# One hybrid decoder step on one core: fetch and split of the head outputs in two threads, whole value transposes, a new order of the column groups, and the inverse's small transfers on ScalarE's queue

## The chip, the core and the metric

The kernel runs on one core of a Trainium2 chip. Its engines work side by side, each through its own list of instructions in order: TensorE (PE, matmuls and transposes into PSUM), VectorE (DVE), ScalarE (ACT), GpSimd (POOL) and SyncE (SP, which here does nothing but issue DMA transfers). The metric is the time of one execution on the device in microseconds; lower is better. Before the change it is 1345.04 us, the median of three runs (1344.74 to 1347.03).

## The reference

One layer of a decoder that runs two mixers side by side on the same input of 2048 channels: RWKV-7 (16 heads of 64) and retention (8 heads of 128). There are 592 tokens: 16 meta tokens and 512 prompt tokens of one sequence, and 8 new tokens for each of 8 running sequences, which bring their own states.

```
z = einsum('btd,dn->btn', x, w_in)                 # 2048 -> 4224 (RWKV) + 4096 (retention) columns
o_a, s_a, shift = _rwkv7_mixer(z[..., :N_A_COLS], ...)   # per token: S <- S*w + (S·-kk) b^T + v k^T;  o = S·r
o_b, s_b = _retention_mixer(z[..., N_A_COLS:], ...)      # S <- g*S + k^T v, rotary q and k, group norm, gate
h = einsum('btc,cd->btd', concat([o_a, o_b]), w_out)     # 2048 -> 2048
y = layer_norm(ALPHA * x + h)
```

Everything is fp32. The new states of both mixers and the last projected row (`shift`) are outputs too.

## The kernel before

**Precision.** The two large products are done in three matmuls each, on a rounded high part and the remainder: `wh*XH`, `wh*XL` and `wl*XH`. ACT makes the high part (`wh<-raw`) and DVE the low part (`wl<-raw,wh`) of every weight chunk of 256 KB. Four such buffer pairs rotate; a chunk is loaded into one of three `raw` buffers by SP.

**Column groups.** The input projection runs over 65 column groups of 128 columns (`units`): one for the low-rank parts, then for each of eight pairs `p` (two RWKV heads, one retention head) the groups A k, r, v, g and B q, k, v, g. A group is four weight chunks, first over tokens 0 to 271 into `bank0`, then over the other 320 into `bank1`: 96 matmuls of 256 to 320 columns, then the next group. Evacuation of a bank (`gen_evac`) applies the token shift or the rotary factors. The rows `f32 ... 128x272` and `128x320` of the profile are these matmuls.

**Work of a pair beside it.** While TensorE goes through the groups, threads (Python generators) put their instructions between its matmuls:
- `gen_a(p)`: decays, keys, and the products of a chunk of 64 tokens; transposes of the values (`zsV`) into `Y` and `ZZ`; then a "bonus" product with `BD` that scales `zsV`.
- `gen_u(p)`: the inverse of a triangular 64 x 64 matrix for each chunk and head. The four 32 x 32 blocks go out to DRAM (`lt_d<-RW`, 4 transfers of 40 KB), come back spread over 120 partitions (`RW<-lt_d`, 3 of 160 KB), are inverted by 62 DVE instructions, and go back the same way (`tt_d<-RW`, 3 of 55 KB; `RW<-tt_d`, 4 of 40 KB).
- `gen_c(p)`: the chain over the nine chunks. Each link is matmul, ACT (`RHS`), matmul, DVE, matmul, DVE, and the next link needs the last result.
- `gen_s(p)`: the eight running sequences. `gen_f(p)`: group norm and gate of the RWKV output. `gen_b(h)`: retention head `h`, with `ron` as its output.

Outputs of pairs 0 to 6 are parked in DRAM (`o_d`). For the output projection `gen_o` fetches them again into five tiles, splits them into `xo` (in `XH`) and `xl`, and marks `o`. The last two, of pair 7, are taken from SBUF. The output projection has four column blocks `n` of 512, sixteen row blocks `k` and five token tiles `t`; for `n = 0` the first `EARLY = 14` row blocks are done for tiles 0 and 1 ahead of the rest (84 matmuls), and the rest of `n = 0` begins only when retention head 7 and the shift rows are done, since it needs their PSUM banks. The first 14 row blocks of `n = 0` take 196 matmuls in all, row block 14 another 14, and then row block 15 (pair 7's RWKV output) is needed.

**What sets the order.** Nothing is scheduled while the kernel runs. A planner (`Order`) keeps, as the program is built, an estimated clock for each engine, for PSUM and SBUF regions and for the DMA path, and places an instruction of a thread when its operands will be ready by the estimate and TensorE has come to that point. The estimates are in `Engine.cost`: before, a DVE instruction costs 68 ns + 1.04 ns a column whatever it is (but for `reciprocal`), an ACT instruction 93 (51 from PSUM) + 0.833. A transfer is taken to land 1300 ns + its bytes at 270 B/ns + 2400 ns (`LAND`) behind its issue. What is placed stays in that order on its engine, and an engine whose next instruction isn't ready waits. All transfers go through SP's list. `take` and `give` hand out three PSUM banks to the threads.

All ACT and DVE instructions of the threads carry line L380 in the profile, matmuls L403, transposes L409, DMA issues L420.

## Time and profile before

| | |
|---|---|
| median of three runs | 1345.04 us (1344.74 to 1347.03) |
| the profiled execution | 1345.04 us; 1343.3 us from its first to its last instruction |
| TensorE busy | 1309.4 us (97%) |
| VectorE busy | 879.8 us (65%) |
| ScalarE busy | 634.4 us (47%) |
| GpSimd busy | 55.3 us (4%) |
| mean DMA rate | 104 GB/s |
| granted TensorE clock | 0.997 |

The profiled execution's time is the median. The busy time of TensorE counts overlapping ends of pipelined matmuls, so how fast it is must be read from the distance between the starts of its instructions. An engine's idle time is listed by what ended it. DMA issues are seen on the queue of the engine that issues them (here SPq), with the time that the issue itself took; when the data landed is seen from who waited for it.

### The profile page before, as it was taken

Reading aid. Unit: us, or ns where it says so; the run is one execution under the profiler, and the core shown is the slowest. Engines: PE = TensorE matmul, PEld = TensorE weight load, DVE = VectorE, ACT = ScalarE, POOL = GpSimd, SP = SyncE. Lnnn points to the kernel's source line nnn. Section 1 sums busy time; section 2 is a strip of 40 time slices with the busy share of each in tenths; the row PEclk is TensorE's granted clock in tenths of the full one; section 3 lists DMA queues with packets and bytes.
Section 4 is the critical chain, followed back from the end, with each engine's and each line's share of the span. In section 5 each row is a group of like instructions: output and inputs, shape, how many; then the busy total and the mean of one; then the engine's idle time right before and its main releaser. Section 6 shows DMA issues by size and latency. Waiting matters only on the chain.

```text
span 1343.3 us, 27153 instructions
## 1 busy us (share of the span) xinstructions
PE 1309.4 (97%) x10488; PEld 1230.2 (92%) x10488; DVE 879.8 (65%) x2168; ACT 634.4 (47%) x1505; POOL 55.3 (4%) x117
## 2 busy tenths in 40 slices
PE   6999999999999999999999999999999998999995
PEld 6999999999999999999999999999999995777774
DVE  5765587658765876587658765876587658634258
ACT  4543654365536553655365536553655375512110
POOL 0000010000000010001000100010001000000002
PEclk9999999999999999999999999999999999999998
DMA  8343234322433243324332433243324356563224
GB/s 244 89 110 84 68 89 120 83 82 74 119 84 83 74 116 86 84 74 114 87 84 74 113 88 85 73 113 86 86 74 114 83 162 191 172 193 118 79 67 145
DMA packets 232344, 139.82 MB, mean 104 GB/s; under 512 B 58668, under 2 KB 212102, under 8 KB 231238
## 3 DMA queue, kind: packets, MB, share of 16 engines
q1 hardware_dynamic: 232214, 138.08, 36.2%
q8 instruction: 82, 1.34, 0.4%
q14 instruction: 48, 0.39, 0.1%
HBM read 119.30 MB, written 18.74 MB: 103 GB/s over the span
## 4 chain that ended last, share of the span: by engine, by line
PE 92%; DVE 5%; issue 1%; ACT 1%; DMA 0%; DVEq 0%; SPq 0%; ACTq 0%
PE bank L403 88%; PE bank L409 4%; DVE RW L380 3%; DVE wl L380 1%; DVE XL L380 1%; DMA RW<-in_x_prompt_dram 0%; DVE SHT L380 0%; ACT XH L380 0%; DVE XH L380 0%; ACT RT L380 0%; DVE RT L380 0%; ACT RSv L380 0%; ACT wh L380 0%; ACT SF L380 0%; ACT RHS L380 0%
## 5 line engine op out<-in xcount | busy, mean ns | idle before, releaser
L403 PE MATMUL bank<-XL,wh 128*128 128x320 f32 (+3 forms) x2080 | 631.3, 303 | 0.0
L403 PE MATMUL bank<-XH,wh 128*128 128x320 f32 (+3 forms) x2080 | 629.6, 303 | 1.2 <-ACT wh L380 1.2
L403 PE MATMUL bank<-XH,wl 128*128 128x320 f32 (+3 forms) x2080 | 626.1, 301 | 0.6 <-DVE wl L380 0.6
L403 PEld LDWEIGHTS bank<-XH,wh 128*128 128x128 f32 x2080 | 391.8, 188 | 3.6 <-ACT wh L380 1.4
L403 PEld LDWEIGHTS bank<-XH,wl 128*128 128x128 f32 x2080 | 392.0, 188 | 2.9 <-DVE wl L380 0.8
L403 PEld LDWEIGHTS bank<-XL,wh 128*128 128x128 f32 x2080 | 391.8, 188 | 2.9
L380 DVE TENSOR_TENSOR wl<-raw,wh 128x512 fp32r<-128x512 f32 x292 | 200.8, 689 | 156.2 <-ACT wh L380 151.8
L380 ACT ACTIVATE wh<-raw 128x512 fp32r<-128x512 f32 x292 | 183.8, 630 | 172.9 <-PE bank L403 145.6
L380 DVE TENSOR_TENSOR RW<-RW 120x84 f32<-120x84 f32 (+26 forms) x544 | 137.9, 256 | 18.5 <-DMA RW<-lt_d 4.1
L403 PE MATMUL bank<-RW 32*32 32x32 f32 (+6 forms) x2000 | 137.0, 239 | 4.8 <-DVE RW L380 4.7
L403 PEld LDWEIGHTS bank<-RW 32*32 32x32 f32 (+4 forms) x2000 | 109.8, 144 | 23.5 <-DVE RW L380 9.7
L380 ACT ACTIVATE RW<-bank 64x256 f32<-64x256 f32 (+8 forms) x218 | 93.2, 438 | 52.8 <-PE bank L403 29.1
L380 ACT ACTIVATE RT<-bank 64x320 f32<-64x320 f32 (+9 forms) x122 | 47.7, 397 | 114.0 <-DVE RT L380 72.6
L403 PE MATMUL bank<-more,XH 128*128 128x512 f32 (+1 forms) x250 | 75.9, 395 | 0.0
L380 ACT ACTIVATE SF<-RW,FT 64x64 f32<-64x64 f32 x144 | 49.4, 343 | 54.7 <-DVE RW L380 52.9
L403 PE MATMUL bank<-wh,XH 128*128 128x512 f32 x157 | 61.8, 396 | 0.0
L403 PE MATMUL bank<-wl,XH 128*128 128x512 f32 (+1 forms) x157 | 61.7, 395 | 0.0
L409 PE MATMUL bank<-CT,RW 128*128 128x128 f32 (+2 forms) x348 | 53.4, 283 | 8.3 <-DMA RW<-in_x_prompt_dram 7.6
L403 PEld LDWEIGHTS bank<-more,XH 128*128 128x128 f32 (+1 forms) x250 | 45.6, 183 | 12.6
L380 ACT ACTIVATE RW<-bank,OMM 128x272 f32<-128x272 f32 (+1 forms) x66 | 33.3, 504 | 45.6 <-PE bank L403 42.9
L403 PE MATMUL bank<-wh,XL 128*128 128x512 f32 x126 | 50.4, 400 | 1.4 <-DVE XL L380 1.4
L409 PEld LDWEIGHTS bank<-CT,RW 128*128 128x128 f32 (+2 forms) x348 | 42.0, 140 | 9.5 <-issue 7.6
(151 smaller groups left out, 1352.9 us busy)
## 6 DMA issues: line engine op xcount, KB each, us to landing
raw<-in_w_in_dram SPq DMA_DIRECT2D x259, 256.0 KB
raw<-in_w_out_dram SPq DMA_DIRECT2D x48, 256.0 KB
CT<-in_w_out_dram SPq DMA_DIRECT2D x30, 256.0 KB
RT<-in_state_ret_dram SPq DMA_DIRECT2D x8, 512.0 KB
out_dram<-RT SPq DMA_DIRECT2D x8, 512.0 KB
RW<-in_x_prompt_dram SPq DMA_DIRECT2D x16, 256.0 KB
out_dram<-RW SPq DMA_DIRECT2D x16, 256.0 KB
RW<-o_d SPq DMA_DIRECT2D x14, 288.0 KB
```

The source lines that it names most:

```text
L380: self.order.submit(Op(self.key, self.cost(name, n, kw, psum), reads, [out], lambda: f(*args, **kw)))
L403: lambda: self.eng.matmul(out, lhsT, rhs, start=start, stop=stop), (passes, move, load, shape, tiles)))
L409: lambda: self.eng.transpose(out, in_, ident), (1, move, _cols(in_) / 1.2, shape, tiles)))
```

## The change

- **Value transposes.** `zsV` was transposed in ten pieces of 64 tokens to 64 partitions of PSUM; now five pieces of 128 tokens go to all 128 partitions, and the even and odd chunks are copied from the two halves. ACT copies go from 9 to 12 a pair for the same elements.
- **Bonus product** as a thread of its own (`gen_bonus`, named X), started when the values are transposed. The next pair's r group and the gate of `gen_f` wait for it. The running sequences (`gen_s`) wait for `V` before they use `Y`.
- **Order of the column groups**: A k, r, then B q, k, v, g, then A v, g; in the last pair A k, r, B q, A v, B k, v, A g, B g.
- **The inverse's 14 small transfers a pair** are issued on ACT's queue. The constant `TI` stays on SP.
- **The planner's estimates**: DVE 82 ns instead of 68, a scan 2.08 ns a column instead of 1.04, ACT 107 and 68 instead of 93 and 51; a transfer on ACT's queue takes 480 ns of ACT and lands 900 ns (`LAND_OWN`) instead of 2400 ns after its bytes.
- **Fetch and split**: `gen_fetch` loads a parked output as soon as its own tile is free; `gen_o` splits.
- **The shift rows** wait for the last evacuation.

No computation is added or left out.

```diff
@@ -36,6 +36,7 @@
 LAND_BIG = 2400.0
+LAND_OWN = 900.0
 LD = 4
...
@@ -44,6 +45,8 @@
 EARLY = 14
+TURNS = "Ak Ar Bq Bk Bv Bg Av Ag"
+TURNS_LAST = "Ak Ar Bq Av Bk Bv Ag Bg"
 KEEP = ("A", 7, "g")
...
@@ -212,17 +215,19 @@
         self.clock[op.eng] = end
-        if op.eng in ("SP", "AQ"):
+        by = op.eng
+        if op.size and op.eng != "PE":
+            by = "SP"
             end = max(end + 1300.0, self.clock["DMA"]) + op.size / 270.0
             self.clock["DMA"] = end
-            end += LAND if op.size < 2e5 else LAND_BIG
+            end += LAND_OWN if op.eng == "ACT" else LAND if op.size < 2e5 else LAND_BIG
         for boxes, w in ((op.reads, False), (op.writes, True)):
...
                     l[:] = [x for x in l if x[6] > t]
-                l.append((p0, p1, c0, c1, w, op.eng, end))
+                l.append((p0, p1, c0, c1, w, by, end))
         op.emit()
...
@@ -356,10 +361,10 @@
         if self.key == "DVE":
-            return 68 + n * (6.3 if name == "reciprocal" else 1.04) + 57 * sum(
+            return 82 + n * {"reciprocal": 6.3, "tensor_tensor_scan": 2.08}.get(name, 1.04) + 57 * sum(
                 _is_ap(kw.get(k)) for k in ("scalar", "scalar1", "scalar2"))
         if self.key == "ACT":
-            return (51 if psum else 93) + n * 0.833 + 93 * sum(_is_ap(kw.get(k)) for k in ("scale", "bias"))
+            return (68 if psum else 107) + n * 0.833 + 93 * sum(_is_ap(kw.get(k)) for k in ("scale", "bias"))
         if kw.get("op") == ALU.pow:
...
@@ -430,7 +435,7 @@
     S = Dma(nc.sync, "SP", od)
-    S2 = Dma(nc.scalar, "AQ", od)
+    S2 = Dma(nc.scalar, "ACT", od)
     until, mark, stage = od.until, od.mark, od.stage
...
@@ -752,16 +757,27 @@
         G.memset(Y[64:128, 1, 9, :], 0.0)
-        for c0, c1 in ((0, 4), (4, 8), (8, 10)):
+        for g0, g1 in ((0, 4), (4, 5)):
             bb, = yield from take()
-            b = bb.rearrange("p (c n) -> p c n", c=4)
-            n = c1 - c0
-            for c in range(c0, c1):
-                T.transpose(b[0:64, c - c0, :], zsV[:, 64 * c:64 * c + 64], ident)
-            act(ZZ[64:128, c0:c1], b[0:64, 0:n].rearrange("p c (h v) -> p c h v", h=2))
-            act(Y[64:128, 0, c0:c1, :], b[0:64, 0:n, 0:64])
-            act(Y[0:64, 1, c0:c1, :], b[0:64, 0:n, 64:128])
+            b = bb.rearrange("p (g n) -> p g n", g=4)
+            for g in range(g0, g1):
+                T.transpose(b[:, g - g0, :], zsV[:, 128 * g:128 * g + 128], ident)
+            for e in range(2):
+                own, cs = b[64 * e:64 * e + 64, 0:g1 - g0], slice(2 * g0 + e, 2 * g1, 2)
+                act(ZZ[64:128, cs], own.rearrange("p g (h v) -> p g h v", h=2))
+                act(Y[64:128, 0, cs, :], own[:, :, 0:64])
+                act(Y[0:64, 1, cs, :], own[:, :, 64:128])
             give(bb)
+        mark(f"V{p}", 1)
+        od.call(lambda: od.start(f"X{p}", gen_bonus(p), 2))
+        yield from until((f"U{p}", 99))
+        b, = yield from take()
+        yield from gen_c(p, b)
+        give(b)
+        od.call(lambda: od.start(f"F{p}", gen_f(p), 2))
+        yield
+
+    def gen_bonus(p):
         yield from hold()
...
@@ -773,13 +789,6 @@
         give(b0, b1)
-        mark(name, 3)
-        yield
-        yield from until((f"U{p}", 99))
-        b, = yield from take()
-        yield from gen_c(p, b)
-        give(b)
-        od.call(lambda: od.start(f"F{p}", gen_f(p), 2))
         yield
...
@@ -812,22 +821,22 @@
             h, q = k // 2, k % 2
-            S.dma_start(out=lt_d[p % 2][k].rearrange("c s t -> s c t"),
+            S2.dma_start(out=lt_d[p % 2][k].rearrange("c s t -> s c t"),
                         in_=LT[64 * h + 32 * q:64 * h + 32 * q + 32, :, 32 * q:32 * q + 32])
...
         for g in range(3):
-            S.dma_start(out=SUB3[40 * g:40 * g + 40], in_=lt_d[p % 2].rearrange("k c s t -> (k c) s t"))
+            S2.dma_start(out=SUB3[40 * g:40 * g + 40], in_=lt_d[p % 2].rearrange("k c s t -> (k c) s t"))
         for j in range(31):
...
         for g in range(3):
-            S.dma_start(out=tt_d[p % 2].rearrange("k (m g) i -> k m g i", g=3)[:, :, g, :], in_=TI[40 * g:40 * g + 40])
+            S2.dma_start(out=tt_d[p % 2].rearrange("k (m g) i -> k m g i", g=3)[:, :, g, :], in_=TI[40 * g:40 * g + 40])
         mark(f"U{p}", 2)
...
             h, q = k // 2, k % 2
-            S.dma_start(out=TT[64 * h + 32 * q:64 * h + 32 * q + 32, :, 32 * q:32 * q + 32],
+            S2.dma_start(out=TT[64 * h + 32 * q:64 * h + 32 * q + 32, :, 32 * q:32 * q + 32],
                         in_=tt_d[p % 2][10 * k:10 * k + 10, 0:32].rearrange("c j i -> j c i"))
...
@@ -879,6 +888,7 @@
         give(tr)
+        yield from until((f"X{p}", 99))
         tt(on, on, zsV[:, 64:640], ALU.add)
...
@@ -908,6 +918,7 @@
         act(RSs, n0[:, 256:384])
+        yield from until((f"V{p}", 1))
         mm(n0[:, 384:512], AR_[:, 1728:1856], Y[:, :, 9, :])
...
@@ -1060,7 +1071,7 @@
                     if half == 0 and p:
-                        yield from until((f"A{p-1}", 1 if s == "k" else 3) if s in "kr" else (f"F{p-1}", 99))
+                        yield from until({"k": (f"A{p-1}", 1), "r": (f"X{p-1}", 99)}.get(s, (f"F{p-1}", 99)))
                     zs, i = {"r": (zsR, 0), "k": (zsK, 1), "v": (zsV, 2), "g": (zsG, 3)}[s]
...
@@ -1094,7 +1105,7 @@
     for p in range(NPAIR):
-        units += [("A", p, s) for s in "krvg"] + [("B", p, s) for s in "qkvg"]
+        units += [(x[0], p, x[1]) for x in (TURNS if p < NPAIR - 1 else TURNS_LAST).split()]
...
@@ -1263,26 +1274,37 @@
+        def gen_fetch():
+
+            for i in range(KO - 2):
+                t, kt = otk[i % 5], korder[i]
+                if t is TA:
+                    yield from until((f"S{NPAIR-1}", 1))
+                elif t is Z0:
+                    yield from until(("evac", 2 * len(units)))
+                else:
+                    yield from until((f"U{NPAIR-1}", 2))
+                if i >= 5:
+                    yield from until(("o", i - 4))
+                yield from until((f"{'F' if kt < 8 else 'B'}{kt % 8}", 99))
+                S.dma_start(out=t[:, 0:576], in_=o_d[kt])
+                mark("fetch", i + 1)
+                yield
+
         def gen_o():
...
-            yield from until((f"U{NPAIR-1}", 2), (f"S{NPAIR-1}", 1), (f"A{NPAIR-1}", 3), ("evac", 2 * len(units) - 8))
-
-            for ki in range(KO + 5):
-                if ki >= 5:
-                    k = ki - 5
+            for k in range(KO):
+                if k < KO - 2:
+                    yield from until(("fetch", k + 1))
                     t = otk[k % 5][:, 0:576]
-                    if k >= KO - 2:
-                        yield from until((f"B{NPAIR-1}", 99), (f"{'F' if k == KO - 1 else 'B'}{NPAIR-1}", 99))
-                        t = Y_[:, 64:640] if k == KO - 1 else ron
-                    yield from until(("event", n_in - 4 + min(3, (640 * k + 639) // TOK // 4) + 1))
-                    act(xo[:, k, 0:576], t)
-                    tt(xl[:, k, 0:512], t[:, 0:512], xo[:, k, 0:512].bitcast(F32), ALU.subtract)
-                    tt(xo[:, k, 576:640], t[:, 512:576], xo[:, k, 512:576].bitcast(F32), ALU.subtract)
-                    mark("o", k + 1)
-                if ki < KO - 2:
-                    kt = korder[ki]
-                    yield from until((f"{'F' if kt < 8 else 'B'}{kt % 8}", 99))
-                    S.dma_start(out=otk[ki % 5][:, 0:576], in_=o_d[kt])
+                else:
+                    yield from until((f"X{NPAIR-1}", 99), (f"B{NPAIR-1}", 99), (f"{'F' if k == KO - 1 else 'B'}{NPAIR-1}", 99))
+                    t = Y_[:, 64:640] if k == KO - 1 else ron
+                yield from until(("event", n_in - 4 + min(3, (640 * k + 639) // TOK // 4) + 1))
+                act(xo[:, k, 0:576], t)
+                tt(xl[:, k, 0:512], t[:, 0:512], xo[:, k, 0:512].bitcast(F32), ALU.subtract)
+                tt(xo[:, k, 576:640], t[:, 512:576], xo[:, k, 512:576].bitcast(F32), ALU.subtract)
+                mark("o", k + 1)
...
@@ -1337,7 +1359,7 @@
         def gen_shift():
-            yield from until((f"B{NPAIR-1}", 99))
+            yield from until((f"B{NPAIR-1}", 99), ("evac", 2 * len(units)))
             rows = SHO.rearrange("p s i -> p (s i)")
...
@@ -1353,6 +1375,7 @@
+        od.start("fetch", gen_fetch(), OPRIO)
         od.start("o", gen_o(), OPRIO)
```

What moves on the engines, at two places. The first is a round of the inverse in an odd pair. Before, SP issues its last transfers among the loads of the weight chunks (`raw`):

```order
L420 DMA raw_100<-in_w_in_dram 128x4x128
L420 DMA tt_d_127<-RW 440x1x32 x2
L420 DMA raw_101<-in_w_in_dram 128x4x128
L420 DMA raw_99<-in_w_in_dram 128x4x128
L420 DMA raw_100<-in_w_in_dram 128x4x128
L420 DMA tt_d_127<-RW 440x1x32
L420 DMA RW<-tt_d_127 32x10x32 x4
```

Now they stand in ACT's list, among the splits (`wh`) and the copies of retention:

```order
L425 DMA tt_d_127<-RW 440x1x32
L385 ACTIVATE RT<-RT 32x128 x2
L385 ACTIVATE wh_104<-raw_101 128x512
L385 ACTIVATE XH<-RT 32x128 x2
L385 ACTIVATE RT<-RT 32x128 x2
L385 ACTIVATE RT<-bank_116 128x320
L425 DMA tt_d_127<-RW 440x1x32
L385 ACTIVATE wh_105<-raw_99 128x512
L425 DMA RW<-tt_d_127 32x10x32 x4
L385 ACTIVATE RW<-bank_115,OMM 128x272
L385 ACTIVATE RW<-bank_115 128x272
```

Between the last store of the round and the loads that need it stands one split in the pairs 1, 3 and 5, six instructions with two splits in the pairs 2, 4 and 6, and two copies of a bank in pair 7. Behind the loads stand the copies of the next bank and the next split.

The second place is TensorE's list where the output projection has begun and the chain of pair 7 isn't finished. Before, these are the rows around the 84th matmul of the output projection (`bank0` and `bank1` with 512 columns; `RW` and `RHS,RW` are the chain, `CT,RT` the transposes of retention head 7, `CT,SHO` the shift rows, `64x64` the end of the chain):

```order
L403 MATMUL bank_115<-wh_105,XL 128x512
L409 MATMUL bank_121<-CT,RT 128x128 x4
L409 MATMUL bank_122<-CT,RT 128x80
L403 MATMUL bank_115<-wl_109,XH 128x512
L403 MATMUL bank_117<-RW 128x128
L403 MATMUL bank_117<-RHS,RW 66x128
L409 MATMUL bank_121<-CT,SHO 33x128
L409 MATMUL bank_121<-CT,SHO 88x128
L403 MATMUL bank_117<-RW 128x128
L409 MATMUL bank_121<-CT,SHO 88x128 x2
L403 MATMUL bank_120<-RW 64x64 x26
```

Now the transposes of head 7 stand behind 5 matmuls of the output projection instead of 83, and the shift rows behind 13 instead of 84:

```order
L408 MATMUL bank_115<-wh_102,XL 128x512
L414 MATMUL bank_121<-CT,RT 128x128 x4
L414 MATMUL bank_122<-CT,RT 128x80
L408 MATMUL bank_115<-wl_106,XH 128x512
L408 MATMUL bank_117<-RW 128x128
L408 MATMUL bank_119<-wh_103,XH 128x512
L408 MATMUL bank_119<-wh_103,XL 128x512
L408 MATMUL bank_119<-wl_107,XH 128x512
L408 MATMUL bank_115<-wh_103,XH 128x512
L408 MATMUL bank_115<-wh_103,XL 128x512
L408 MATMUL bank_115<-wl_107,XH 128x512
L408 MATMUL bank_118<-RW 128x128
```

The end of the chain (`64x64`) stands behind 84 of these matmuls before and behind 140 now; the transposes after the group norm of pair 7 behind 118 and behind 174.

## The prediction

> **What bounds the kernel now.** I read the page first, then the stages, then TensorE's waits. The page has TensorE busy all the time, and it owns the chain that ended last:
>
> ```profile
> span 1343.3 us, 27153 instructions
> PE 1309.4 (97%) x10488; PEld 1230.2 (92%) x10488; DVE 879.8 (65%) x2168; ACT 634.4 (47%) x1505; POOL 55.3 (4%) x117
> PE 92%; DVE 5%; issue 1%; ACT 1%; DMA 0%; DVEq 0%; SPq 0%; ACTq 0%
> ```
>
> So a gain must come from TensorE's own work or from places where TensorE waits; ACT, with 47%, has room, but only on average. By stages (span, then busy time of PE, PEld, DVE, ACT, POOL):
>
> ```profile
> 550.00:600.00 50.00, 49.55 (x463) 47.17 (x462) 37.72 (x94) 33.03 (x90) 1.57 (x3) 1.00 0.24 68
> 1100.00:1150.00 50.00, 43.32 (x271) 32.65 (x270) 42.41 (x93) 32.65 (x71) 4.13 (x4) 1.00 0.62 183
> 1150.00:1200.00 50.00, 50.00 (x218) 39.54 (x217) 25.35 (x40) 17.90 (x30) 0.00 (x0) 1.00 0.67 213
> ```
>
> A pair in the middle loses 0.45 us, the stretch where the last pair's chain meets the output projection 6.68 us, the output projection nothing. The waits of TensorE over the whole span, and then those between 1100 and 1150 us:
>
> ```profile
> PE bank L403 <- DVE RW L380: 4.7, 8, 1.1
> PE bank L403 <- ACT RHS L380: 2.8, 3, 1.3
> PE bank L403 <- DVE XL L380: 1.4, 3, 0.9
> PE bank L409 <- ACT RT L380: 0.4, 1, 0.4
> ...
> PE bank L403 <- DVE RW L380: 2.1, 2, 1.1
> ```
>
> The second set has the other three rows unchanged. So 2.1 + 2.8 + 1.4 + 0.4 = 6.7 us are lost in that stretch, and 4.7 - 2.1 = 2.6 us in 8 - 2 = 6 waits before it, one a pair, 0.44 us each. What the start and the end cost (loading x, the last norm and store) the change leaves as it is. The profiled execution's own time is 1345.04 us, 1.7 us more than its span, and is the median; sums below start from it.
>
> **The change, part by part.**
>
> *Value transposes.* What five transposes fewer a pair save is read from distances between starts, in pair 5's beginning:
>
> ```profile
> 619.38 0.60 PE L409 MATMUL bank<-CT,RW 128*128 128x128 f32 x4
> 619.73 0.36 PE L403 MATMUL bank<-XH,wl 128*128 128x258 f32 x1
> 619.93 0.28 PE L403 MATMUL bank<-XH,wh 128*128 128x258 f32 x1
> ...
> 622.38 0.60 PE L409 MATMUL bank<-CT,RW 128*64 128x128 f32 x4
> 622.74 0.36 PE L403 MATMUL bank<-XH,wh 128*128 128x258 f32 x1
> 622.94 0.28 PE L403 MATMUL bank<-XL,wh 128*128 128x258 f32 x1
> 623.06 0.28 PE L403 MATMUL bank<-XH,wl 128*128 128x258 f32 x1
> ```
>
> Four transposes of 64 columns and the matmul behind them take 622.94 - 622.38 = 0.56 us; a 258-column matmul alone takes 623.06 - 622.94 = 0.12; so the four cost 0.44, or 0.11 each. Four with 128 columns cost 619.93 - 619.38 - 0.12 = 0.43: the same. Ten become five: 5 x 0.11 = 0.55 us a pair, 8 x 0.55 = 4.4 us. All of it is TensorE's time in stages where it is 99 to 100% busy, so it counts in full, as long as nothing else comes to bound the pair. The three copies more on ACT (12 for 9) lie under TensorE's work (ACT's share is 47%).
>
> *The planner's price of a scan.* The wait in each middle pair has this in front of it:
>
> ```profile
> 577.82 1.52 DVE L380 TENSOR_TENSOR_SCAN RW<-CT,RW 128x657 f32<-128x657 f32 x1
> ...
> 712.43 1.52 DVE L380 TENSOR_TENSOR_SCAN RW<-CT,RW 128x657 f32<-128x657 f32 x1
> ...
> 580.98 0.28 DVE L380 TENSOR_TENSOR RW<-bank,N 64x128 f32<-64x128 f32 x1
> ...
> 581.32 0.49 PE L403 MATMUL bank<-RW 128*128 128x128 f32 x2 [0.45 <-DVE RW L380]
> ```
>
> The second scan row, from the next pair, gives the period: 712.43 - 577.82 = 134.6 us. The scan took 1.52 us; the old price is 68 + 657 x 1.04 = 751 ns, so the planner put the chain's matmul some 0.77 us too early behind it. The new price is 82 + 657 x 2.08 = 1449 ns. TensorE has matmuls of the column groups to do meanwhile, so the 2.6 us go; bounds 0 (another instruction is as badly priced) and 2.6. I take 2.6.
>
> *Last pair and output projection.* Before, 83 of the 84 early matmuls stand ahead of head 7's transposes, and the chain's last links wait one after another with nothing to put between. DVE is full there:
>
> ```profile
> 1120.00:1130.00 10.00, 7.48 (x45) 5.12 (x43) 9.79 (x22) 6.47 (x14) 1.75 (x2) 1.00 0.52 155
> ```
>
> Now head 7 is done earlier (its q group is third in the pair, and its transposes stand behind 5 output matmuls), the banks of tiles 2 to 4 come free, and the chain's links have 140 matmuls around them instead of 84. One takes 0.23 us:
>
> ```profile
> 1321.01 0.40 PE L403 MATMUL bank<-wh,XL 128*128 128x512 f32 x1
> 1321.24 0.40 PE L403 MATMUL bank<-wl,XH 128*128 128x512 f32 x1
> ```
>
> 56 x 0.23 = 12.9 us of fill for 2.1 + 2.8 + 0.4 = 5.3 us of waits for the chain and the shift rows. I take those as gone. The 1.4 us for XL I keep: the split can only begin when the last column group has read XH, which no earlier fetch alters. Bounds 0 and 6.7, taken 5.3.
>
> What is late next? Row block 15 needs pair 7's output. From the copy of the chain's result to the end of its split:
>
> ```profile
> 1140.43 0.60 ACT L380 ACTIVATE RW<-bank 128x512 f32<-128x512 f32 x1 [1.51 <-PE bank L403]
> ...
> 1155.19 0.69 DVE L380 TENSOR_TENSOR XL<-RW,XH 128x512 fp32r<-128x512 f32 x1
> ```
>
> that is 1155.88 - 1140.43 = 15.5 us. Before, 210 - 84 = 126 output matmuls (29 us) covered it. Now 70 are left, 70 x 0.23 = 16.1 us, and 0.55 for five transposes among them: 16.7. The margin is 1.2 us. Without it TensorE stands for what the norm is late; I take 0, at worst 2 us.
>
> *The inverse's transfers on ACT.* What SP paid:
>
> ```profile
> L420 SPq DMA_DIRECT2D lt_d<-RW x32: 331/452/1143, 77.6 to 1023.4; - x32
> L420 SPq DMA_DIRECT2D RW<-lt_d x24: 307/326/328, 81.2 to 1026.3; - x24
> L420 SPq DMA_DIRECT2D RW<-tt_d x32: 332/450/464, 122.9 to 1068.1; - x32
> L420 SPq DMA_DIRECT2D tt_d<-RW x24: 788/814/1352, 113.4 to 1063.5; - x24
> SPq L420 <- DMA tt_d<-RW: 15.6, 8, 2.2
> SPq L420 <- DMA lt_d<-RW: 0.8, 3, 0.3
> ```
>
> A pair's 14 issues come to 4 x 0.452 + 3 x 0.326 + 4 x 0.450 + 3 x 0.814 = 7.0 us of ACT, which makes its 634 us 690. The waits, 2.0 us a pair for `tt_d` (at most 2.2) and at most 0.3 for `lt_d`, now hold ACT. Queued behind them are splits, copies of the two projection banks and the chain's `RHS` and `SF`. How long may a split be late?
>
> ```profile
> 534.93 0.63 ACT L380 ACTIVATE wh<-raw 128x512 fp32r<-128x512 f32 x1 [1.12 <-PE bank L403]
> 536.69 0.63 ACT L380 ACTIVATE wh<-raw 128x512 fp32r<-128x512 f32 x1 [1.12 <-PE bank L403]
> 537.35 0.69 DVE L380 TENSOR_TENSOR wl<-raw,wh 128x512 fp32r<-128x512 f32 x1 [0.64 <-ACT wh L380]
> ```
>
> TensorE frees a buffer every 1.76 us and comes back to it three chunks later, after 5.3 us; the split takes 0.63 + 0.69 = 1.3 us and 0.1 between. So 3.9 us are to spare. The worst hop is `tt_d`, 2.2 of wait and 4 x 0.45 = 1.8 of issue, 4.0 us, less what a split between them uses up. That is 0.1 us over for each of 8 pairs, 0.8 us; the other hop (0.3 + 3 x 0.326 = 1.3 us) is covered. Bounds 0 and 0.8 by these rows; I take 0.8. SP loses waits among the weight loads, but no wait of TensorE names a weight load, so I credit nothing.
>
> *Bonus thread, order of the groups, separate fetch.* The bonus product has the group A k of the next pair (some 17 us) before A r needs its tile; no instruction is added. The values now come as the seventh group, right before the chain, where before they lay ready early; TensorE has groups to do until then. I take 0, between -1 and +2 us (one wait of 0.25 us a pair).
>
> *Sum.* 1345.0 - 4.4 - 2.6 - 5.3 + 0.8 = 1333.5 us.
>
> **The rivals.**
>
> A: *The stretch at the end keeps its waits.* For it: DVE's 9.79 of 10 us there: a full engine isn't helped by more fill. Against: the same DVE work is now spread over 12.9 us more of matmuls, and head 7 lies earlier. Price: the 5.3 us stay, and of the rest nothing changes: 1338.8 us.
>
> B: *ACT's wait eats the gain.* The point is 3.9 us from the last split on time. For it: in the first pair DVE stood 4.1 us for such a transfer:
>
> ```profile
> 88.29 0.87 DVE L380 TENSOR_TENSOR RW<-RW 120x31 f32<-120x31 f32 x4 [4.11 <-DMA RW<-lt_d]
> ```
>
> A wait as long on ACT, with 1.8 us of issue, is 5.9 us, 2.0 us over. In one hop a pair: 8 x 2.0 = 16 us in place of the 0.8, so 1345.0 - 12.3 + 16 = 1348.7 us. In both hops it would be 1365. It decides from 12.3 / 8 = 1.5 us over the margin a pair. Against: that wait had two weight loads of 256 KB queued ahead, and at the ACT hops SP never waited over 2.2 us.
>
> C: *Two queues hold each other up at the issue.* So far SP alone issues. If each of the four `RW<-tt_d` issues on ACT lasted one SP issue longer, that is 4 x 0.45 = 1.8 us a pair beyond the 0.1, and 1345.0 - 12.3 + 8 x 1.9 = 1347.9 us. For it: no row excludes it. Against: SP is left with a weight load of 0.4 us or so every 134.6 / 32 = 4.2 us, so most ACT issues meet none. The Trainium skill (Perfetto Trace Analysis, "DMA Instruction — HWDGE (DVE, Sync)") states the rule behind this: an issuing sequencer waits for its semaphores first and then locks the descriptor generator for its exclusive use. With one issuer before, no run here shows it yet.
>
> D: *Nothing to be seen.* The new prices are only other errors: each middle pair gets one wait of 0.5 to 1 us elsewhere (8 x 0.75 = 6 us), and the end keeps its waits: 1338.8 + 6 = 1344.8 us. For it: 14 ns more on each DVE instruction is far from exact. Against: with prices half as good there was one wait a pair.
>
> **How the numbers follow.** Forecast 50%, A 25%, D 13%, B 7%, C 5%. The forecast's own range is 1331 (XL's 1.4 us and ACT's 0.8 go too) to 1337.5 (2 us for row block 15 and 2 for the new order come). For 8 in 10 the range goes down to 1330, since transfers freed of SP's list may gain a little, and up past A to 1345. A measurement here tells about 0.2%, 2.7 us, from no change. Faster by more than that (below 1342.3): forecast, A and a third of D, 0.79. Within it: the rest of D and a third of C, 0.11. Slower: B and the rest of C, 0.10.
>
> **What would show it.** In the profile after: TensorE's waits for DVE RW near zero in the middle pairs, and a stretch of 10 us without `[... <-DVE RW]` behind the scan; 40 transposes fewer, all of 128 columns; a pair's period shorter by about 1 us; PE's idle time of 6.7 us around the last chain down to 1 to 2 us; ACT's waits for `tt_d` near 2 us a pair, with no wait of PE for `wh` or `wl`. Wrong it is if PE waits for `wh` or `wl` in each pair (B or C), if PE still waits for RHS at the end (A), or if row block 15 makes a new gap before the second column block.

## The result, and the profile after

The changed kernel took 1323.24 us (median of four runs, 1322.62 to 1324.24), the kernel before beside it 1345.15 us (1344.74 to 1347.03): ratio 0.9835, 95% interval 0.9818 to 0.9852. That is 21.9 us less, where 11.5 were forecast. The direction was right, the size was not; the time lies below the range of 1330 to 1345.

The page of the changed kernel (span; busy time and share of each engine; the chain that ended last by engine):

```profile
span 1322.0 us, 27007 instructions
PE 1297.2 (98%) x10448; PEld 1225.3 (93%) x10448; DVE 881.1 (67%) x2168; ACT 634.6 (48%) x1529; POOL 56.8 (4%) x117
PE 92%; DVE 4%; DMA 1%; ACT 1%; issue 1%; POOL 1%; ACTq 0%; SPq 0%; DVEq 0%; POOLq 0%
```

Its stages, the same three stretches as before (span, then busy time of PE, PEld, DVE, ACT, POOL):

```profile
550.00:600.00 50.00, 50.00 (x463) 48.84 (x463) 33.76 (x89) 31.09 (x89) 0.20 (x1) 1.00 0.30 82
1100.00:1150.00 50.00, 49.73 (x288) 39.14 (x287) 36.19 (x73) 31.49 (x66) 2.00 (x2) 1.00 0.62 195
1150.00:1200.00 50.00, 50.00 (x217) 39.61 (x216) 18.21 (x28) 10.35 (x17) 0.00 (x0) 1.00 0.51 161
```

And all waits of its TensorE that the view lists:

```profile
PE bank L414 <- DMA RW<-in_x_prompt_dram: 7.9, 2, 7.6
PE bank L408 <- ACT wh L385: 1.2, 1, 1.2
PE bank L408 <- DVE wl L385: 0.9, 2, 0.6
PE bank L414 <- DVE XL L385: 0.6, 1, 0.6
```

What is left is the program's start and one wait of 0.26 us for `wl` at 1111.5 us. The rows for `DVE RW` (4.7 us), `ACT RHS` (2.8), `ACT RT` and the projection's `XL` are gone; the stretch around the last chain, which lost 6.68 us, loses 0.27.

The length of a pair is read from TensorE itself: every kernel has the same 6240 products of the input projection, 96 for each column group, so the first product of a pair is found by counting. The first and the last of the eight pairs begin, before (with one product more, to show the distance of two starts), at

```profile
35.81 0.28 PE L403 MATMUL bank<-XH,wh 128*128 128x272 f32 x1
966.63 0.29 PE L403 MATMUL bank<-XH,wh 128*128 128x272 f32 x1
966.75 0.29 PE L403 MATMUL bank<-XL,wh 128*128 128x272 f32 x1
```

and after, at

```profile
36.91 0.28 PE L408 MATMUL bank<-XH,wh 128*128 128x272 f32 x1
955.65 0.38 PE L408 MATMUL bank<-XH,wh 128*128 128x272 f32 x1
```

So the span's 21.3 us divide as follows.

| stretch | before | after | measured | forecast |
|---|---|---|---|---|
| start to the first pair | 35.8 | 36.9 | +1.1 | 0 |
| seven pairs | 930.8 | 918.7 | -12.1 | -(7 x 0.55 + 5 x 0.44) = -6.1 |
| last pair's start to the end | 376.6 | 366.3 | -10.3 | -(0.55 + 0.44 + 5.3) = -6.3 |

(The forecast's +0.8 for ACT's queue was spread over the pairs; of the six waits behind a scan, five lie in the seven pairs and one in the last.) From the third to the seventh, the pairs took 134.6 us each; now they take 132.6 to 132.9. VectorE's scan, from which the prediction took the period, is no good ruler after the change: it stands 131.9 and 133.6 us apart in turn, since its place within the pair changes.

### The profile page after: what moved, and what is told of

It is laid out like the page before. It is cut to its first block, busy times and chain, and to the rows that moved or that the text cites. A ratio compares the mean times of both kernels' runs of the same rounds, so it can differ in the third digit from the quotient of the medians.

```text
span 1322.0 us, 27007 instructions
## 1 busy us (share of the span) xinstructions
PE 1297.2 (98%) x10448; PEld 1225.3 (93%) x10448; DVE 881.1 (67%) x2168; ACT 634.6 (48%) x1529; POOL 56.8 (4%) x117
## 4 chain that ended last, share of the span: by engine, by line
PE 92%; DVE 4%; DMA 1%; ACT 1%; issue 1%; POOL 1%; ACTq 0%; SPq 0%; DVEq 0%; POOLq 0%
PE bank L408 89%; PE bank L414 4%; DVE RW L385 2%; DVE XL L385 1%; POOL MOM L385 1%; DMA RW<-in_x_prompt_dram 0%; DVE SHT L385 0%; DVE wl L385 0%; DMA tt_d<-RW 0%; DVE RT L385 0%; DVE MOM L385 0%; ACT RT L385 0%; ACT XH L385 0%; ACT RW L385 0%; ACT wh L385 0%
## 5 line engine op out<-in xcount | busy, mean ns | idle before, releaser
L408 PE MATMUL bank<-RW 32*32 32x32 f32 (+6 forms) x2000 | 133.8, 237 | 0.0
L385 ACT ACTIVATE RW<-bank 64x64 f32<-64x64 f32 (+8 forms) x242 | 96.2, 411 | 52.2 <-PE bank L408 25.3
L414 PE MATMUL bank<-CT,RW 128*128 128x128 f32 (+3 forms) x308 | 47.4, 281 | 8.5 <-DMA RW<-in_x_prompt_dram 7.9
L414 PEld LDWEIGHTS bank<-CT,RW 128*128 128x128 f32 (+3 forms) x308 | 38.1, 146 | 9.9 <-issue 7.6
```

Source lines behind the costliest of these rows:

```text
L385: self.order.submit(Op(self.key, self.cost(name, n, kw, psum), reads, [out], lambda: f(*args, **kw)))
L408: lambda: self.eng.matmul(out, lhsT, rhs, start=start, stop=stop), (passes, move, load, shape, tiles)))
L414: lambda: self.eng.transpose(out, in_, ident), (1, move, _cols(in_) / 1.2, shape, tiles)))
```

## What the middle of the program gained, row by row

The third to the seventh pair fell from 134.62 us to 132.78 on average, 1.84 us each. Two parts were foreseen. The transposes take 0.55 us less. The wait behind the scan is gone; it cost more than its listed 0.44. From the start of the wide product ahead of it (580.57) to the waiting one (581.32, shown above) 0.75 us passed, where two such starts stand 0.15 apart, so 0.60. The listed wait only begins where the product ahead ends, 0.30 after its start, though in a full stream the next one starts before that end. The two products ahead:

```profile
580.42 0.31 PE L403 MATMUL bank<-XH,wl 128*128 128x320 f32 x1
580.57 0.30 PE L403 MATMUL bank<-XH,wh 128*128 128x320 f32 x1
```

A third part was not foreseen. Before, a group of eight products of 64 rows (16 passes) was cut by one wide product in the third and each later pair, six times:

```profile
605.02 0.93 PE L403 MATMUL bank<-RW 64*128 64x128 f32 x10
605.88 0.39 PE L403 MATMUL bank<-XH,wh 128*128 128x272 f32 x1
606.20 0.71 PE L403 MATMUL bank<-RW 64*128 64x128 f32 x6
606.84 0.39 PE L403 MATMUL bank<-XL,wh 128*128 128x272 f32 x1
```

After, all 16 such groups stand whole:

```profile
604.45 1.16 PE L408 MATMUL bank<-RW 64*128 64x128 f32 x16
605.54 0.41 PE L408 MATMUL bank<-XH,wl 128*128 128x320 f32 x1
```

By distances between starts the pieces take 0.86 and 0.64 us and the wide product between them 0.32, together 1.82. The whole group takes 1.09 and such a wide product in the stream 0.12 (966.63 to 966.75, above), together 1.21. So a cut costs 0.61 us, and 0.55 + 0.60 + 0.61 = 1.76 of the 1.84 have a name. The first two pairs, which had neither this wait nor this cut, fell by 2.4 and 0.5 us; beyond the 0.55 each, I can't assign these.

## The experiments

All kernels compute the whole reference. They were run in several sessions, in which the kernel before took 1345.1 to 1346.7 us, so a difference of up to 1.5 us between two sessions can be the session's. Three kinds were run: one edit taken back from the change, one edit alone in the kernel before, and a ladder between the two.

| edit taken back | us | ratio to before, 95% | against the change | seven pairs | last pair's start to the end |
|---|---|---|---|---|---|
| none (the change) | 1323.24 | 0.9818 to 0.9852 | | 918.7 | 366.3 |
| order of groups, all pairs | 1357.70 | 1.0070 to 1.0100 | +34.5 | 944.5 | 373.4 |
| ACT's queue | 1333.98 | 0.9897 to 0.9927 | +10.7 | 923.9 | 371.9 |
| bonus's thread | 1333.00 | 0.9888 to 0.9921 | +9.8 | 919.1 | 374.5 |
| all prices | 1331.24 | 0.9876 to 0.9909 | +8.0 | 922.9 | 369.4 |
| fetching thread | 1329.87 | 0.9869 to 0.9899 | +6.6 | 918.8 | 372.7 |
| whole transposes | 1329.42 | 0.9858 to 0.9887 | +6.2 | 924.7 | 366.4 |
| order in the last pair | 1326.68 | 0.9846 to 0.9872 | +3.4 | 919.3 | 370.0 |

The last two columns are lengths in one trace of each kernel, found by counting products as above. They say where an edit acts: the fetching thread, the last pair's order and the bonus's thread at the end, the transposes in the pairs.

Without the last row, which the one for all pairs contains, these come to 76 us, over three times the gain of the whole.

| edit alone in the kernel before | us | ratio, 95% |
|---|---|---|
| the scan's price | 1378.52 | 1.0231 to 1.0259 |
| order of groups (not the last pair) | 1359.84 | 1.0088 to 1.0118 |
| whole transposes | 1348.48 | 1.0007 to 1.0025 |

None of these makes it faster.

### Prices taken back

```diff
-            return 82 + n * {"reciprocal": 6.3, "tensor_tensor_scan": 2.08}.get(name, 1.04) + 57 * sum(
+            return 68 + n * (6.3 if name == "reciprocal" else 1.04) + 57 * sum(
-            return (68 if psum else 107) + n * 0.833 + ...
+            return (51 if psum else 93) + n * 0.833 + ...
```

> The change with the planner's old prices of VectorE and ScalarE operations, all else kept (against 1323.2 us of the change). My theory: the prices carry only the wait on the scan, which costs 0.60 us of each pair's pitch before and nothing after, so the time rises by 4.8 us, to 1328.0. By the size that the prediction took (6 x 0.44) it rises by 2.6, to 1325.8. Rival: the new order of the work alone already sets the reader of the scan far enough behind it, and the prices carry nothing: 1323.2. The eight-product groups of 64-row products stay whole in the written order under all three, so nothing is expected from those.

1332.08 us, 0.9895 (0.9878 to 0.9911). One of its five executions, the traced one, took 3395 us and is left out. The same kernel once more:

> The change with the planner's old prices once more (1332.1 us before, with no usable trace). Theory 1: the wait on the scan is back, 0.44 to 0.6 us in six or seven pairs, 3 to 5 of the 8.8 us. Theory 2: the old prices draw another of many orders: no wait on the scan; the loss stands in a few places, as waits at the start or the end or a pitch over 133.5.

1331.24 us, 0.9892 (0.9876 to 0.9909). TensorE's waits for VectorE's `RW` in its trace:

```profile
PE bank L408 <- DVE RW L385: 0.7, 2, 0.4
```

Both lie after 1100 us; none is behind a scan, and the pairs of the middle take 133.0 to 133.3 us. So the wait on the scan went with the new order of the work, not with the scan's price: theory 2.

### Old order of groups, and the old order in the last pair alone

```diff
-TURNS = "Ak Ar Bq Bk Bv Bg Av Ag"
+TURNS = "Ak Ar Av Ag Bq Bk Bv Bg"
-TURNS_LAST = "Ak Ar Bq Av Bk Bv Ag Bg"
+TURNS_LAST = "Ak Ar Av Ag Bq Bk Bv Bg"
```

> The change with the old order of the column groups in every pair, the last one too. My theory: the middle of the program does not change (the pitch of a pair stays at 132.7 us), but the last pair's groups again leave TensorE without work there, so most of the 6.7 us of waits at the end come back: 1328 to 1330. Rival 1: the separate fetching thread carries the end, and the order of groups is worth under 1 us: 1323 to 1324. Rival 2: the order also moves the pitch of the pairs, which the first scan-to-scan distances would show (over 133.5 us).

1357.70 us, 1.0085 (1.0070 to 1.0100): all three theories were far too low. In every second pair TensorE has gaps at one place:

```profile
620.29 0.66 PE L414 MATMUL bank<-CT,RW 128*128 128x128 f32 x4 [1.36 <-DVE RW L385]
...
623.93 0.58 PE L408 MATMUL bank<-XH,wh 128*128 128x258 f32 x1 [1.41 <-ACT RW L385]
```

The wide product of the next column group waits as well, for a copy by ACT, so TensorE had nothing to do in the gap. These pairs take 141.7 to 142.4 us, the ones between them 130.3 to 131.1.

```diff
-TURNS_LAST = "Ak Ar Bq Av Bk Bv Ag Bg"
+TURNS_LAST = TURNS
```

> The change with the last pair's groups in the same new order as the other pairs (g of A ahead of nothing, v and g of A last). The middle stays as it is under every theory (pitch 132.7 us). Theory 1: the last pair's value and gate groups then come too late for the value transposes and the bonus, and the end waits for them: 5 us or more, 1328 to 1333. Theory 2: the end's gain comes from the fetching thread and the queue: 1323 to 1325.

1326.68 us, 0.9859 (0.9846 to 0.9872): the middle pairs as in the change (132.9 us), between the two theories. From the last pair's start on it takes 3.7 us more than the change, so the last pair's own order is worth 3.4 to 3.7 us.

### The inverse's transfers back on SP

```diff
-            S2.dma_start(out=lt_d[p % 2][k]...
+            S.dma_start(out=lt_d[p % 2][k]...
```

(and the same for the other three of `gen_u`)

> The change with the inverse's small transfers issued by the SP queue again. My theory: the queue carries nothing, in either direction, since TensorE does not wait for what these transfers bring: 1323.2, within 0.7. By the prediction's term for the transfers on ScalarE's queue (+0.8 of the change) it would be 1322.4; if their earlier landing was what made the end's gain, up to 1328.

1333.98 us, 0.9912 (0.9897 to 0.9927), outside all that I expected. TensorE now waits for weights once in each pair:

```profile
PE bank L408 <- ACT wh L385: 4.4, 8, 1.2
PE bank L408 <- DVE wl L385: 2.1, 8, 0.6
```

The middle pairs take 133.8 us instead of 132.8. SP's queue in that kernel, where a pair's weight loads (`raw`) go out behind the transfers:

```profile
625.49 14.61 SPq L425 DMA_DIRECT2D raw<-in_w_in_dram  x5
```

and in the changed kernel, where the loads begin at once:

```profile
621.59 18.28 SPq L425 DMA_DIRECT2D raw<-in_w_in_dram  x7
```

The loads start 625.49 - 621.59 = 3.9 us later, of which 2.0 are the pair's own later begin (559.3 for 557.3). But TensorE doesn't wait for the data. It waits for a split:

```profile
634.40 0.39 PE L408 MATMUL bank<-XH,wh 128*128 128x272 f32 x1 [0.44 <-ACT wh L385]
```

That split begins at 633.73, and the DMA view from 631.3 to 633.7 us shows no packet, so every load issued by then had landed. ACT's list in that kernel has the split behind two steps of retention, for which ACT stood idle 1.65 and 0.88 us:

```profile
632.05 0.21 ACT L385 ACTIVATE RT<-RT 128x16 f32<-128x16 f32 x1 [1.65 <-DVE RT L385]
633.14 0.69 ACT L385 ACTIVATE RT<-bank,CT 128x512 f32<-128x512 f32 x1 [0.88 <-PE bank L414]
633.73 0.62 ACT L385 ACTIVATE wh<-raw 128x512 fp32r<-128x512 f32 x1
```

In the changed kernel it stands ahead of them:

```profile
627.84 0.63 ACT L385 ACTIVATE wh<-raw 128x512 fp32r<-128x512 f32 x1
629.47 0.22 ACT L385 ACTIVATE RT<-RT 128x16 f32<-128x16 f32 x1 [0.99 <-DVE RT L385]
```

So the queue matters for the place that the splits get in the written order; that the planner takes the loads behind SP's transfers to land later would explain it, but is not shown. That is 5.2 us of the 10.7, in the seven pairs. Another 5.6 us lie behind the last pair's start; around the last chain six waits of 0.22 to 0.45 us come back.

### The cut groups

```diff
             for c in range(c0, c1):
+                if c == c0 + 2:
+                    yield
+                    now = od.clock["PE"]
+                    while od.clock["PE"] < now + 300:
+                        yield
```

> The change with each of its 16 whole groups of eight 64-row products (two in each pair) cut into two groups of four, with wide products of 128 rows between. Nothing else is changed by hand. My theory: each entry into and exit from the 64-row form costs, from the groups of 10 and 6 passes before against the whole ones of 16 after, 0.41 us more in the groups and 0.1 in the wide products beside them, so 16 cuts cost 16 x 0.45 to 0.5 = 7 to 8 us: 1330 to 1331. Rival: the form's change costs nothing by itself and the groups were short of operands where they were cut: 1323 to 1324.

1331.42 us, 0.9891 (0.9876 to 0.9906): +8.2 us, and no new waits (TensorE's listed waits sum to 10.5 us, as in the change's 10.6). The middle pairs take 133.58 us instead of 132.78, 0.80 for two cuts, so 0.40 each. The rows say the same:

```profile
607.74 0.71 PE L408 MATMUL bank<-RW 64*128 64x128 f32 x8
608.38 0.41 PE L408 MATMUL bank<-XH,wl 128*128 128x320 f32 x1
608.72 0.71 PE L408 MATMUL bank<-RW 64*128 64x128 f32 x8
609.37 0.41 PE L408 MATMUL bank<-XH,wh 128*128 128x320 f32 x1
```

From 607.74 to 609.37 are 1.63 us, where the whole group and a wide product in the stream take 1.09 + 0.15. Sixteen cuts are 6.4 us of the 8.2; the last pair has 1.7 us beyond its two cuts. The cut of the kernel before, into 10 and 6 passes, was dearer, 0.61 by its rows, so its six cuts are 3.7 us. The Trainium skill (TensorEngine Tiling (Array Packing), "Key Properties") says that a change of the tiling mode drains TensorE; this run agrees in that a cut costs time with nothing waiting, 0.40 us, but doesn't show the draining itself.

### The scan's price alone

```diff
-            return 68 + n * (6.3 if name == "reciprocal" else 1.04) + 57 * sum(
+            return 68 + n * {"reciprocal": 6.3, "tensor_tensor_scan": 2.08}.get(name, 1.04) + 57 * sum(
```

> The kernel before with one thing changed: the planner prices a scan on VectorE at 2.08 ns an element instead of 1.04. In the written order the six cut groups of 64-row products stand whole again. My theory, two gains: the wait on the scan goes (0.60 us of each pair's pitch, x 8 = 4.8) and the six cuts go (the run with 16 cuts added cost 8.2 us, 0.51 each: 3.1), together 7.9 us less than before: 1338.4 beside 1346.3. By the prediction's size: 2.6 less, 1343.7. Rival: the price only moves the wait to another product: 1346.

1378.52 us, 1.0245 (1.0231 to 1.0259): slower by 32 us with a truer price and no group cut. The pairs now take 139.8 us, and TensorE's waits are of another kind:

```profile
PE bank L409 <- DVE RW L380: 10.3, 16, 1.4
PE bank L403 <- ACT RW L380: 7.6, 7, 1.1
```

One such place, with its matmuls:

```profile
635.13 0.66 PE L409 MATMUL bank<-CT,RW 128*128 128x128 f32 x4 [1.36 <-DVE RW L380]
...
638.72 0.58 PE L403 MATMUL bank<-XH,wh 128*128 128x258 f32 x1 [1.14 <-ACT RW L380]
639.10 0.42 PE L403 MATMUL bank<-XL,wh 128*128 128x258 f32 x1
639.32 0.42 PE L403 MATMUL bank<-XH,wl 128*128 128x258 f32 x1
```

and in stretches of 3 us (PE busy, then the granted clock):

```profile
632.00:635.00 3.00, 1.77 (x14) 1.00 0.39 110
635.00:638.00 3.00, 2.00 (x10) 0.77 0.63 138
638.00:641.00 3.00, 2.28 (x10) 0.50 0.70 214
641.00:644.00 3.00, 3.00 (x18) 0.59 0.31 108
```

In 9 us TensorE stands idle for 1.23 + 1.00 + 0.72 = 2.95 us, and the granted clock falls to 0.50: starts of the 258-column products are 0.22 us apart (639.10 to 639.32) where they were 0.12. The clock costs at most another 3 x (0.23 + 0.50 + 0.41) = 3.4 us, less where a slow stretch is also idle. So at most 6.3 us, less the 0.60 of the old wait and the 0.61 of the cut, 5.1 a pair: close to what the pair grew (139.8 - 134.6 = 5.2).

### The whole transposes, alone and taken back

The short form of the edit, alone in the kernel before:

```diff
-        for c0, c1 in ((0, 4), (4, 8), (8, 10)):
+        for g0, g1 in ((0, 4), (4, 5)):
...
-                T.transpose(b[0:64, c - c0, :], zsV[:, 64 * c:64 * c + 64], ident)
+                T.transpose(b[:, g - g0, :], zsV[:, 128 * g:128 * g + 128], ident)
```

> The kernel before with one thing changed: the five whole value transposes of each pair in place of ten half ones. My theory: 40 transposes less on TensorE at 0.11 us each, 4.4 us, and five of the six cut groups of 64-row products stand whole in the written order, 2.5 us: 6.9 less than before, 1339.4 beside 1346.3. By the prediction alone: 4.4 less, 1341.9. Rival: VectorE or ScalarE sets the pair's pitch and TensorE's saved time becomes waits: 1345 to 1346.

1348.48 us, 1.0016 (1.0007 to 1.0025). The fourth to seventh pairs fell to 134.0 us, but waits on ACT's `RHS` came in (some 0.25 us in each of five pairs), the second pair met gaps of 0.93, 0.29 and 1.26 us (it takes 138.2 us, before 131.3), and the last chain kept its waits. So TensorE's time was saved and given back in waits of a new order. With the same edit reversed in the change:

> The change with the ten half value transposes of each pair in place of the five whole ones; thread of the bonus, order of groups, prices and queue as in the change (1323.2 us). Theory 1 (the prediction's term): 40 transposes more at 0.11 us, 4.4 us: 1327.6, and no waits of TensorE that the change doesn't have. Theory 2, after the runs that undid one edit each and cost twice to five times their term (8.8, 10.7 and 34.5 us): any other length of a pair's work makes the planner write another order with waits of its own: over 1329, with waits in every pair. Theory 3: the transposes are covered: 1323 to 1325.

1329.42 us, 0.9873 (0.9858 to 0.9887): +6.2. The seven pairs are 6.0 us longer, with one wait of 0.6 us in one of them, and the end is unchanged. In the third and the seventh pair the difference is 0.54 and 0.52 us, the 0.55 of the prediction's rows; the others have more. Theory 1's 4.4 us is most of it; 1.8 us lie in the redrawn order.

### The fetching thread and the bonus's thread taken back

```diff
-        od.start("fetch", gen_fetch(), OPRIO)
...
-                    yield from until(("fetch", k + 1))
+            yield from until((f"U{NPAIR-1}", 2), (f"S{NPAIR-1}", 1), (f"X{NPAIR-1}", 99), ("evac", 2 * len(units)))
+                if ki < KO - 2: S.dma_start(out=otk[ki % 5][:, 0:576], in_=o_d[kt])
```

> The change with the one old thread that fetches the output rows and splits them, its transfers behind its own splits again. Theory 1, from the traces: the order of the last pair's groups and the fetching thread share the end's gain of 6.7 us; without the thread the first products of the output projection wait for their rows again: 1326 to 1330. Theory 2: the thread changes nothing, since the rows are there in time under the new order: 1323 to 1324. If the planner's order breaks elsewhere, as it did with the old order of groups, pairs in the middle would be longer than 132.7 us and the time over 1330.

1329.87 us, 0.9884 (0.9869 to 0.9899): theory 1. The seven pairs are unchanged (918.8 us, in the change 918.7). The one thread now fetches nothing before the last evacuation, where the kernel before waited for eight evacuations fewer: its fifth tile, `Z0`, serves the evacuations of the A groups, and in the last pair's new order one of these is the last group but one. So the output projection's first product comes 8.0 us after the last one of the input projection, which starts at 1087.85:

```profile
1095.88 0.47 PE L408 MATMUL bank<-wh,XH 128*128 128x512 f32 x1
```

In the change it comes 0.14 us after (1088.68), in the kernel before 0.15:

```profile
1088.82 0.40 PE L408 MATMUL bank<-wh,XH 128*128 128x512 f32 x1
```

In the 8.0 us stand the last chain, head 7's transposes and the shift rows, with three waits on VectorE (0.38, 0.42, 0.72 us) from 1088.9 to 1092.0, and the granted clock is at 0.50 for 3 us behind them.

```diff
-        od.call(lambda: od.start(f"X{p}", gen_bonus(p), 2))
+        yield from gen_bonus(p)
+        mark(f"X{p}", 99)
```

> The change with the bonus (two products and their evictions) in the pair's own thread again, ahead of the chunks, instead of in a thread of its own; all else kept. Theory 1 (the prediction's term): 0, so 1323.2, between -1 and +2. Theory 2: it is the thread of its own that lets the next pair's groups of r and k leave their banks early; without it their wide products stall, as in the run with the old order of groups: over 1330, with waits of TensorE in every pair.

1333.00 us, 0.9905 (0.9888 to 0.9921): none of the stalls in the middle that theory 2 wanted: the seven pairs take 919.1 us, in the change 918.7. The loss lies behind the last pair's start, 374.5 us for 366.3, with waits of 0.86 us at 1079 and 1.11 us at 1099, and a clock of 0.86 from 1080 to 1090. Neither theory; see the ladder.

### The order alone, and the ladder

```diff
-        units += [("A", p, s) for s in "krvg"] + [("B", p, s) for s in "qkvg"]
+        units += [(x[0], p, x[1]) for x in ("Ak Ar Bq Bk Bv Bg Av Ag" if p < NPAIR - 1 else "Ak Ar Av Ag Bq Bk Bv Bg").split()]
```

> The kernel before with one thing changed: in all pairs but the last the column groups stand in the new order (k and r of A, the four of B, v and g of A). Theory 1: this order alone puts work that waits for nothing where the next pair's groups of r, v and g waited for the pair before, so the pair's pitch drops from 134.6 to about 133.5 (the waits on the scan and the six cuts go; the ten transposes stay): 1346.3 - 7 x 1.0 = 1339. Theory 2: the order without the inverse's transfers on another queue runs into late weights (the run with only the queue undone has 133.8 a pair and 0.4 to 0.6 us of waits for weights in each): 1343 or more. Theory 3: as the scan's price alone, it gives waits of 2.5 us in a pair and a lower granted clock behind them: over 1360.

1359.84 us, 1.0103 (1.0088 to 1.0118): between theories 2 and 3. Two pairs have a wait for weights of 0.44 us. The seven pairs take 6.1 us more than before, and what follows 8.8 us more; there, behind gaps of 0.89 and 1.58 us at 1030 to 1033, the clock stands at 0.50 for over 6 us.

The other rungs are the changed kernel less what it still lacks: first order, queue and old prices; then the new prices; then the bonus's thread. These three have the one thread that waits for the last evacuation, and their output projections begin 6.8 to 8.6 us after the last input product.

> The run with order, prices and queue together (1333.5), with the old prices: the kernel before with the order of groups and the queue alone. If the prices are what the order needs (the order alone gave 1359.8): 1350 or more. If the queue is what it needs: 1333 to 1337. If both: between.

1343.14 us, 0.9983 (0.9973 to 0.9992): between, so the order needs both the queue and the prices, as far as this run can tell: it has the last pair's new order too.

> The change without the whole transposes, the thread of the bonus and the fetching thread: the kernel before with the new order of groups, the new prices and the inverse's transfers on ScalarE's queue. The prediction's sizes would add up: prices -2.6, queue +0.8, order 0: 1344.5 beside 1346.4. Theory 1: these three edits need each other (the order alone gave 1359.8, the scan's price alone 1378.5) and together they already free TensorE of most waits in the pairs: pitch 133.4 to 134.3 with nearly no listed wait, and the end's waits remain: 1334 to 1341. Theory 2: without the thread of the bonus the wide products of the next pair still stall: over 1350.

1333.50 us, 0.9904 (0.9888 to 0.9921): theory 1. The middle pairs take 133.0 to 133.5 us, and behind the start no wait of 0.25 us or more is left before 1090 us. There stand three waits (0.37, 0.77, 0.49), and the clock falls as above:

```profile
1092.00:1095.00 3.00, 1.85 (x13) 1.00 0.80 246
1095.00:1098.00 3.00, 2.50 (x10) 0.58 1.04 394
1098.00:1101.00 3.00, 3.00 (x19) 0.50 0.52 151
```

> The run before this one (order, prices, queue) with the bonus in a thread of its own; against the change it lacks the whole transposes and the fetching thread. Theory 1, from the run that took the fetching thread alone from the change (+6.6) and the one that took the transposes alone (+6.2): these two act in different places, so they add: 1323.2 + 12.8 = 1336. Theory 2: the edits only count together with the bonus's thread and this is the same as the run before this one. By the prediction's sizes: 1344.5.

1335.63 us, 0.9921 (0.9906 to 0.9936): theory 1.

| rung | us | step | seven pairs | last pair's start to the end |
|---|---|---|---|---|
| before | 1345.1 to 1346.7 | | 930.8 | 376.6 |
| + order of groups | 1359.8 | +13 to +15 | 936.9 | 385.4 |
| + ACT's queue, last pair's order | 1343.1 | -16.7 | 931.2 | 373.2 |
| + prices | 1333.5 | -9.6 | 922.5 | 374.2 |
| + bonus's thread | 1335.6 | +2.1 | 924.1 | 371.9 |
| + fetching thread | 1329.4 | -6.2 | 924.7 | 366.4 |
| + whole transposes | 1323.2 | -6.2 | 918.7 | 366.3 |

The bonus's thread is worth +2.1 here and -9.8 when it is the last to be put in. So what an edit is worth depends on the others. The last two rungs are an exception: the fetching thread is worth 6.2 us without the whole transposes and 6.6 with them, and the transposes 5.8 (1335.6 to 1329.9) without the fetching thread and 6.2 with it. One acts at the end only and the other in the pairs.

### Other prices on the same edits

The prices split: scan alone new; VectorE's new, ScalarE's old; ScalarE's and the scan's new, VectorE's fixed part old.

```diff
-            return 82 + n * {...}
+            return 68 + n * {...}
-            return (68 if psum else 107) + n * 0.833 + ...
+            return (51 if psum else 93) + n * 0.833 + ...
```

> The change with only the scan's new price; the fixed parts of VectorE's and ScalarE's prices (82, 68, 107 ns) back at 68, 51 and 93. Theory 1: the scan's price carries the 8.8 us that undoing all prices cost, so 1323.2 to 1324. Theory 2: the fixed parts, which count in some 3600 instructions, carry it: 1331 or more. Theory 3: they share it.

1328.18 us, 0.9865 (0.9850 to 0.9879): between theories 1 and 2.

> The change with ScalarE's fixed parts back at 51 and 93 ns, VectorE's new prices kept (82, and the scan's). With both engines' fixed parts back the time was 1328.2, with a pitch of 132.6 and the loss at the program's start and end. If VectorE's fixed part carries those 5 us: 1323 to 1324; if ScalarE's does: 1328; if any other set of prices only draws another of many nearly equal orders: anywhere from 1321 to 1332, with the pitch at 132 to 134 and the difference at the start, the end or in single waits.

1326.57 us, 0.9856 (0.9841 to 0.9871).

> The change with VectorE's fixed part back at 68 ns, ScalarE's new prices (68, 107) and the scan's kept. The same three outcomes as for the run with ScalarE's fixed parts back, with the two engines exchanged: 1323 to 1324 if ScalarE's fixed part carries the 5 us, 1328 if VectorE's does, 1321 to 1332 if each set draws another order.

1329.89 us, 0.9883 (0.9869 to 0.9898).

The third outcome of the last two: five sets of prices on the same edits give 1323.2, 1326.6, 1328.2, 1329.9 and 1331.2 us, and neither engine's fixed part carries the difference. Their middle pairs take 132.6 to 133.3 us on average where the change has 132.8, and they have single waits of 0.4 to 1.5 us at changing places: in the first pairs, around 1030 or 1070 us, or at the last chain. So redrawing the order by other prices alone moves the time by up to 8 us, and the size of a single term below that can be trusted only where the trace shows that the rest of the program kept its lengths, as it does for the fetching thread and the last pair's order. None of the kernels run is faster than the change.

## Why the prediction was right and wrong

- **Bound by TensorE, gain where it works or waits**: right. The stages stay full, the chain stays 92% TensorE, and the gain lies in its work and its waits.
- **Transposes, -4.4**: right in mechanism; by the rows 0.55 a pair, and taken back 0.52 to 0.54 in two pairs. Over the whole program, taking them back costs 6.2 us, since the order is redrawn. Alone in the kernel before they gained nothing.
- **The scan, -2.6**: the wait went, but two things in this step failed. It was mis-sized: 6 x 0.60 = 3.6 us by distances of starts, because a wait's listed length leaves out the time by which the next product would have overlapped the one ahead. And "the planner put the chain's matmul some 0.77 us too early" gave the price as the cure: with the old prices in the change the wait is gone too, and the new price alone costs 32 us, since "TensorE has matmuls of the column groups to do meanwhile" doesn't hold in the order that this price draws there: the next column group's products wait as well (1.14 us for a copy by ACT).
- **Last pair, -5.3**: the waits went, but the term was short. From the last pair's start on 10.3 us went, with 0.55 + 0.60 + 0.61 for the transposes, the wait behind the scan and the cut, so 8.5 for 5.3; the 1.4 us of `XL` that I kept did go. The last pair's order carries 3.4 to 3.7. The fetching thread is worth 6.2 and 6.6, all of it there, and I had put "separate fetch" at 0 because "no instruction is added": in the new order it is what lets the output projection begin at once. Without ACT's queue or the bonus's thread 5.6 and 8.2 of the end are lost again. How much the "56 x 0.23 = 12.9 us of fill" carry by themselves, no run shows. No gap came for row block 15.
- **ACT's queue, +0.8**: wrong in sign. The failed step is "SP loses waits among the weight loads, but no wait of TensorE names a weight load, so I credit nothing". True of the kernel before; in the new order with the transfers on SP, TensorE waits for a split of the weights in each pair, 5.2 us in the seven pairs, and loses 5.6 us more at the end (10.7 by the times). The loads had landed; the split stood late in ACT's list. ACT's cost did not show: no wait of TensorE for `wh` or `wl` in the pairs.
- **Order, bonus's thread, separate fetch: 0, -1 to +2**: wrong; this is the step that failed most. The new order decides where all the other waits fall. Without it the rest costs 34.5 us more; order (the last pair's too), queue and prices together are -12.5, of which 8.3 lie in the seven pairs. For these three the forecast had -1.8 and a share of the 5.3.
- **What the sum lacked**: the cut groups (6 x 0.61 = 3.7 us) were nowhere in it.
- **The sum as a whole**: each edit was priced at its place in the old order. In this program every edit redraws the order, so the terms were not parts of one sum. That the direction came out right rests on the stages (idle places at the end and in each pair), not on the single terms.

Of the rivals, A fell (no wait for `RHS` is left), and D (no new waits in the pairs). B and C fell as well. A wait like B's did come, ACT idle for 5.04 us until `tt_d` at 531.8, but once, and TensorE lost nothing by it. The issue times on ACT's queue, in the changed kernel (least, median and greatest ns):

```profile
L425 ACTq DMA_DIRECT2D RW<-tt_d x32: 326/479/1578, 120.8 to 1063.4; - x32
```

The median is 29 ns above SP's 450; only the greatest, 1578 for 464, looks like C, and not often enough to cost anything. The rule of the Trainium skill that spoke for C (Perfetto Trace Analysis, "DMA Instruction — HWDGE (DVE, Sync)") is not contradicted by that row, which doesn't say how often the two queues met.

Still open: 1.8 us in the first two pairs, and why the planner's order stops the next column group in some draws and not in others. The 1.1 us at the start are the granted clock of the profiled execution, which fell before the first pair in this one and not in the one before (at most 0.06 x 10 + 0.11 x 10 = 1.7 us); the kernel without the fetching thread, with the same instructions up to there, kept 1.00 and reached the first pair at 35.5 us instead of 36.9:

```profile
10.00:20.00 10.00, 7.90 (x49) 0.94 1.06 329
20.00:30.00 10.00, 9.42 (x76) 0.89 0.63 189
```
